# Another order for the seven quadrant products of a feed-forward layer on Trainium2

## The chip, the core and the metric

The kernel runs on one core of a Trainium2 chip. Five engines work side by side, each with its own stream of instructions: TensorE (PE in the profile; its weight loads are PEld), VectorE (DVE), ScalarE (ACT), GpSimd (POOL) and SyncE (SP), which here issues the transfers between HBM and the on-chip memory (SBUF). Matrix products land in PSUM, in banks of 128 x 512 floats. The metric is the device time of one execution in microseconds (us), and lower is better.

## The reference, cut to what matters

The program is one layer of an encoder over two independent sequences of 512 tokens with 1024 features: a state-space branch, a differential attention and a cross attention side by side, a gated sum of the three, and a gated feed-forward network. The change touches the last of these alone:

```python
x = x + merged @ p['w_out'][l]
xn2 = _rmsnorm(x, p['norm_ffn'][l])
gate, up = jnp.split(xn2 @ p['w_ffn_in'][l], 2, axis=-1)
return x + (jax.nn.silu(gate) * up) @ p['w_ffn_out'][l]
```

The hidden width is 2816, that is 22 tiles of 128. Everything is float32.

## The kernel before, in words

**Precision.** TensorE multiplies float32 values rounded to a shorter form. To keep float32 accuracy each operand is split into a high part (`split`, L128: a cast on ScalarE) and a low part (L129: the difference, on VectorE), and each product takes three matmuls: high x high, high x low, low x high. In the profile the moving halves are `th` and `tl`, the weight halves `wh` and `wl`.

**Quadrants.** The feed-forward products are computed two by two blocks at a time with seven block products instead of eight (Winograd's form of Strassen's method). For a hidden tile i the weights are A11 and A12 (two halves of the gate weights) and A21 and A22 (two halves of the up weights); the block sums are S1 = A21 + A22, S2 = S1 − A11, S3 = A11 − A21 and S4 = A12 − S2. The columns are the two sequences. The moving operands were split and summed earlier into seven slots, and `SEVEN` (L1006) pairs each weight block with its slot and sets the order of the products. One product of 128 x 512 is 4 k-steps x 3 = 12 matmuls.

**FF1** is the loop over the 22 hidden tiles. `weights4` (L939 to L970) loads the two weight tiles of i (buffers `wf`), splits A11 and A12 together and A22 alone, has POOL form the four sums (L959 to L962, S1 and S2 in one buffer `ws`, S3 and S4 in another, both of the four rotating `ld` buffers), and splits S12 and S34. S12 and S34 each have one pair of `wh`/`wl` buffers to themselves, so their split for tile i + 1 waits until the products of tile i that read them are over; A11/A12 and A22 share another two pairs in the same way. `products` (L1008) issues the matmuls: for i = 0 six products fill six banks together and the seventh follows; for i = 1 to 20 one product after another; for i = 21 the k loop is outermost, so that seven banks fill together, 21 matmuls per k-step. PSUM has six banks for products (`bkmm`) and two others (`bktr`), of which one takes the seventh product where seven fill together. A bank is free again when its last reader is done.

`quadrants` (L1041) combines the seven products p with sums on VectorE, all recorded at L1038: u2 = S2's product + p1 (p1 is ScalarE's copy of A11's product), c11 = A12's + p1, u3 = S3's + u2, u4 = S1's + u2, c22 = S1's + u3, c21 = A22's + u3, c12 = S4's + u4. c11 and c12 are the gate for the two sequences, c21 and c22 the up half. S1's bank is read twice. Then each sequence goes through the gate: VectorE multiplies by the norm factor (L1090), ScalarE takes tanh (L1091), POOL scales the up half (L1092), VectorE finishes (L1093, L1094), and the tile goes out to HBM (`aD`, L1095).

Beside this, from i = 1 to 18, the loop prepares pieces of the second layer's weights: raw weights are loaded, split, summed on POOL (L424 to L427) and split again, and written to HBM as `wD`.

**The turn to FF2.** At i = 21 the first two pairs of activation tiles are loaded again (`act_pair`, L1054: `fa` at L1057 and `fb` at L1058, in the same four `ld` buffers as the weight sums) and summed (`quad_sums`, L909, L911 and L912 on VectorE, L910 on POOL), then split.

**FF2** is 12 visits (`VISITS`), each to one row pair of outputs and a range of activation pairs, accumulating seven banks over the pairs; each pair is one pass of 21 matmuls with weights loaded from `wD` in two pieces (`prepared`, L1117, issued at L1126: A11, A12, A22 are 384 KB; S3, S2, S4, S1 are 512 KB). After a visit `quadrants` combines the banks and POOL adds the results to y (L1149); visits 0 to 3 also load x1 into y (L1139).

**Order.** TensorE keeps the program's order from i = 21 to the end of FF2. Elsewhere, and on all other engines, a scheduler that simulates the program chooses the order of the instructions on each engine, and of SP's transfers, so that a change of the program order also moves instructions that the edit doesn't name.

Of the kernel before, what the change touches and what calls it, by code (L numbers as in the profile page):

```python
# [14 lines left out]
ALU = mybir.AluOpType  # L15
# [5 lines left out]
L = 512  # L21
# [46 lines left out]
def encoder(ctx: ExitStack, tc: tile.TileContext, a, out):  # L68
    nc = tc.nc
    V, S, PO, PE = nc.vector, nc.scalar, nc.gpsimd, InOrder(tc, nc.tensor)  # L70
# [11 lines left out]
    def open_tags(es, side=None, **tags):  # L82

        for tag, n in tags.items():
            pools[tag] = es.enter_context(tc.tile_pool(name=tag, bufs=n, side=side, reuse_waits="tile"))
# [17 lines left out]
    def bank(tag="mm"):  # L103
        return pools[tag].tile([P, 512], F32, tag=tag, name="bk" + tag)

    def aux():
        return bank("tr")
# [29 lines left out]
    def weight(src, n=DM, tag=None):  # L137
        nonlocal last_w, last_s
        wf = wp.tile([P, DM], F32, tag="wf", name="wf")
        last_w = nc.sync.dma_start(wf[:, :n], src)  # L140
        wh, wl = (slot(tag, dt=F32R, name=n_) if tag else wp.tile([P, DM], F32R, tag=n_, name=n_) for n_ in ("wh", "wl"))
        last_s = split(wh[:, :n], wl[:, :n], wf[:, :n])
        return wh, wl
# [37 lines left out]
    def rstd(acc, n, nt=4):  # L181


        ss = aux()
        for t in range(nt):
            PE.matmul(ss[:, t : t + 1], acc[:, t * P : (t + 1) * P], onec[:, 0:1], start=(t == 0), stop=(t == nt - 1))
        return factor(ss, n, nt)
# [92 lines left out]
    @contextmanager  # L280
    def yielding(sp):

        with tc.issue_after(sp[0].ins), tc.issue_after(sp[1].ins):
            yield
# [145 lines left out]
    def half_piece(behind_=()):  # L430
        with ExitStack() as es_:
            for i_ in behind_:
                es_.enter_context(tc.issue_after(i_.ins))
            return next(prep, None)
# [189 lines left out]
    for i in range(-AHEAD, len(steps) + 1):  # L624
        if i + AHEAD < len(steps):
            h, s, lt = steps[i + AHEAD]
# [12 lines left out]
        if 0 <= i < len(steps):  # L639
            h, s, lt = steps[i]  # L640
# [8 lines left out]
        if i > 0 and steps[i - 1][2] == 3:  # L649
            h, s, _ = steps[i - 1]  # L650
# [318 lines left out]
    for i in range(3):  # L969
        for m in (i, i + 4):  # L970
            x1[m] = slot("x1", name=f"x1_{m}")
            w = weight(a["w_out"][m])
# [24 lines left out]
    def product(ps, w, o, ks=range(4)):  # L997
        wh, wl = w
        for k in ks:
            th, tl = ops[k]  # L1000
            ws_ = slice(k * P, (k + 1) * P)
            PE.matmul(ps, wh[:, ws_], th[:, o], start=(k == 0), stop=False)
            PE.matmul(ps, wh[:, ws_], tl[:, o], start=False, stop=False)
            PE.matmul(ps, wl[:, ws_], th[:, o], start=False, stop=(k == 3))

    SEVEN = (("A11", 0), ("S2", 4), ("A12", 1), ("S3", 5), ("S1", 3), ("A22", 6), ("S4", 2))  # L1006

    def products(i, w):  # L1008


        if i == 0:
            ps = [bank() for _ in range(6)]
            for j, k in ((0, 0), (0, 1), (1, 0), (1, 1), (0, 2), (1, 2), (0, 3), (1, 3)):
                for p_, (nm, o) in zip(ps, SEVEN):
                    if nm[0] == "AS"[j]:
                        product(p_, w[nm], o, (k,))
            yield from ps
            last = bank()
            product(last, w["S4"], 2)
            yield last  # L1020
        elif i == KFF - 1:
            ps = [bank() for _ in range(6)] + [aux()]
            for k in range(4):
                for p_, (nm, o) in zip(ps, SEVEN):
                    product(p_, w[nm], o, (k,))
            yield from ps
        else:
            for nm, o in SEVEN:
                p_ = bank()
                product(p_, w[nm], o)  # L1030
                yield p_
# [3 lines left out]
    def summed(tag, p_, other, bufs=1):  # L1035
        nonlocal last_sum
        t_ = (rp if tag == "nsq" else ap2).tile([P, L], F32, tag=tag, name=tag, bufs=bufs)
        last_sum = V.tensor_tensor(out=t_, in0=p_, in1=other, op=ALU.add)  # L1038
        return t_

    def quadrants(ps, p0, other=("up", "gf")):  # L1041

        p1 = ap2.tile([P, L], F32, tag="p1", name="p1")
        S.copy(p1, p0)
        u2 = summed("u2", next(ps), p1)
        c11 = summed("gf", next(ps), p1, 2)
        u3 = summed("u3", next(ps), u2)
        p5 = next(ps)
        u4 = summed("p1", p5, u2)
        c22 = summed("up", p5, u3, 2)  # L1050
        c21 = summed(other[0], next(ps), u3, 2)
        return c11, summed(other[1], next(ps), u4, 2), c21, c22

    def act_pair(p, tag="ts"):  # L1054

        xa_, xb_ = slot("ld", name="fa"), slot("ld", name="fb")
        nc.sync.dma_start(xa_, aD[2 * p])  # L1057
        nc.sync.dma_start(xb_, aD[2 * p + 1])  # L1058
        return xa_, xb_, quad_sums(xa_, xb_, tag)

    for i in range(KFF):
        w = res0
        if i > 0:
            wg = weights4(i)
            with yielding(last_q):
                w = next(wg)
            next(wg)
            next(wg)
        if i == 1:
            prep = prepare(pes, pieces[NPREP[1] :])  # L1070
            next(prep)
        elif i == KFF - 3:
            assert next(prep, None) is None
            pes.close()
            open_tags(fes, side="right", tsa=1, tsb=1)
        if i == KFF - 1:
            acts = [act_pair(0, "tsa"), act_pair(1, "tsb")]
            PE.on = True

        ps = products(i, w)  # L1080
        p0 = next(ps)
        if i == 0:
            for s in range(NS):
                _, bc = rstd(accs[s], DM)
                S.copy(accs[s], bc)
        gf0, gf1, up0, up1 = quadrants(ps, p0)
        ac = ap2.tile([P, NT], F32, tag="ac", name="ac")
        for s, gf, up in ((0, gf0, up0), (1, gf1, up1)):
            cs = slice(s * L, (s + 1) * L)
            V.tensor_tensor(out=gf, in0=gf, in1=accs[s], op=ALU.mult)  # L1090
            last_t = S.activation(out=ac[:, cs], in_=gf, func=AF.Tanh, scale=0.5)  # L1091
            PO.tensor_tensor(out=up, in0=up, in1=accs[s], op=ALU.mult)  # L1092
            V.scalar_tensor_tensor(out=ac[:, cs], in0=ac[:, cs], scalar=1.0, in1=gf, op0=ALU.add, op1=ALU.mult)  # L1093
            V.tensor_tensor(out=ac[:, cs], in0=ac[:, cs], in1=up, op=ALU.mult)  # L1094
        nc.sync.dma_start(aD[i], ac)  # L1095
        if 1 <= i < KFF - 3:
            half_piece((last_t, last_sum))
# [33 lines left out]
    for v, (m, lo_, hi_) in enumerate(VISITS):  # L1131
        ps = [bank() for _ in range(6)] + [aux()]
        for p in range(lo_, hi_):
            th, tl = pairs[p]
            w = prepared(m, p)
            if v < 4 and p == 1:
                with queued():
                    for t in (m, m + 4):
                        nc.sync.dma_start(y[t], x1D[t])  # L1139
            for p_, (nm, o) in zip(ps, SEVEN):  # L1140
                wh, wl = w[nm]
                PE.matmul(p_, wh, th[:, o], start=(p == lo_), stop=False)
                PE.matmul(p_, wh, tl[:, o], start=False, stop=False)
                PE.matmul(p_, wl, th[:, o], start=False, stop=(p == hi_ - 1))
        ps = iter(ps)
        c11, c12, c21, c22 = quadrants(ps, next(ps), ("nsq", "nsq"))
        for c_, t, s in ((c11, 0, 0), (c22, 4, 1), (c21, 4, 0), (c12, 0, 1)):
            yv = y[m + t][:, s * L : (s + 1) * L]
            PO.tensor_tensor(out=yv, in0=yv, in1=c_, op=ALU.add)  # L1149
        if v == 0:  # L1150
            with tc.issue_after(last_sum.ins):
                pairs.append(quad_split(2, *nxt))
        elif v == 1:
            with tc.issue_after(last_sum.ins):
                pair_in()
        for _ in range({3: 2, 4: 1, 6: 1, 7: 1}.get(v, 0)):
            pair_in()
        if v == 8:

            r0, r1 = quad_room(NPAIR)  # L1160
            r2 = slot("ts", [P, 4, L], F32R, name="r2")
            room = [(r0[:, 2 * i : 2 * i + 2], r1[:, 2 * i : 2 * i + 2]) for i in range(3)] + [(r2[:, 0:2], r2[:, 2:4])]
            ah, al = [], []
            for i in range(2 * NPAIR, KFF):
                ac = slot("ld", name="fl")
                nc.sync.dma_start(ac, aD[i])
                th, tl = (r_.rearrange("p a n -> p (a n)") for r_ in room[i - 2 * NPAIR])
                split(th, tl, ac, scale=0.5)
                ah.append(th)
                al.append(tl)  # L1170
# [472 lines left out]
```

## Time and profile before

| what | value |
|---|---|
| median of 3 runs | 1638.84 us (1638.17 to 1641.62) |
| the profiled execution | 1642.78 us, span 1641.0 us |
| TensorE busy | 1594.0 us, 97% of the span, 7812 matmuls |
| VectorE busy | 1176.3 us, 72% |
| ScalarE busy | 635.9 us, 39% |
| POOL busy | 551.3 us, 34% |
| mean granted TensorE clock | 0.99 |
| DMA, mean over the span | 158 GB/s |

The span is the profiled execution's own length on the core, and the time of that execution stands above it by what lies around the program. A line of the timeline gives the start in us, the duration, the engine and line (L1038 is line 1038 of the kernel), the operation, and output <- inputs with buffer numbers left out; square brackets give the idle time before the instruction and what ended it. "x2" marks instructions drawn together. A line of the waits gives who waited for whom, then the total in us, the number of times, and the longest. The granted clock is the share of full speed that TensorE was allowed.

### The profile page before, as it was taken

Reading aid. Unit: us, or ns where it says so; the run is one execution under the profiler, and the core shown is the slowest. Engines: PE = TensorE matmul, PEld = TensorE weight load, DVE = VectorE, ACT = ScalarE, POOL = GpSimd, SP = SyncE. Lnnn points to the kernel's source line nnn. Section 1 sums busy time; section 2 is a strip of 40 time slices with the busy share of each in tenths; the row PEclk is TensorE's granted clock in tenths of the full one; section 3 lists DMA queues with packets and bytes.
Section 4 is the critical chain, followed back from the end, with each engine's and each line's share of the span. In section 5 each row is a group of like instructions: output and inputs, shape, how many; then the busy total and the mean of one; then the engine's idle time right before and its main releaser. Section 6 shows DMA issues by size and latency. Waiting matters only on the chain.

```text
span 1641.0 us, 21700 instructions
## 1 busy us (share of the span) xinstructions
PE 1594.0 (97%) x7812; PEld 1315.9 (80%) x7812; DVE 1176.3 (72%) x1860; ACT 635.9 (39%) x1132; POOL 551.3 (34%) x444
## 2 busy tenths in 40 slices
PE   7999999899999999999999999999999998999997
PEld 5788787788898778777767887888888887888887
DVE  7957898246764676767567659998988887986445
ACT  6534323245553355564232444332333332331122
POOL 0001100000232221200565245666676664444242
PEclk9999999999999999999999999999999999999999
DMA  9354532746764110144785442333333334897632
GB/s 361 129 164 147 154 133 94 234 156 216 245 234 141 52 59 21 50 150 163 247 299 180 154 141 70 114 114 120 119 107 118 106 113 136 299 315 244 209 118 103
DMA packets 109354, 259.60 MB, mean 158 GB/s; under 512 B 14016, under 2 KB 42432, under 8 KB 109248
## 3 DMA queue, kind: packets, MB, share of 16 engines
q1 hardware_dynamic: 109248, 258.23, 46.6%
q8 instruction: 61, 1.00, 0.3%
q14 instruction: 45, 0.37, 0.1%
HBM read 174.85 MB, written 83.33 MB: 157 GB/s over the span
## 4 chain that ended last, share of the span: by engine, by line
PE 85%; DVE 6%; issue 3%; POOL 2%; DMA 2%; ACT 1%; SPq 0%; DVEq 0%; POOLq 0%; ACTq 0%
PE bkmm L61 74%; PE bktr L61 3%; PE bksc L61 2%; PE bkoo L61 2%; PE bktr L64 2%; PE bktr L1480 1%; DVE wl L129 1%; POOL mg L726 1%; PE bktr L1451 1%; DVE xt L243 0%; POOL up L1092 0%; DMA yt<-bD 0%; PE bktr L1419 0%; DMA c_r<-cD 0%; DVE tl L129 0%
## 5 line engine op out<-in xcount | busy, mean ns | idle before, releaser
L61 PE MATMUL bkmm<-xh,wh 128*128 128x512 f32 x640 | 255.9, 400 | 1.2 <-ACT wh L128 1.2
L61 PE MATMUL bkmm<-xh,wl 128*128 128x512 f32 x640 | 251.3, 393 | 2.3 <-DVE wl L129 2.3
L61 PE MATMUL bkmm<-xl,wh 128*128 128x512 f32 x640 | 251.1, 392 | 0.0
L61 PE MATMUL bkmm<-th,wl 128*128 128x512 f32 (+1 forms) x621 | 241.8, 390 | 4.8 <-DVE wl L129 4.8
L61 PE MATMUL bkmm<-th,wh 128*128 128x512 f32 (+1 forms) x621 | 241.6, 389 | 1.3 <-ACT th L128 1.3
L61 PE MATMUL bkmm<-tl,wh 128*128 128x512 f32 (+1 forms) x621 | 241.6, 389 | 0.2 <-DVE tl L129 0.2
L129 DVE TENSOR_TENSOR wl<-wf,wh 128x1024 fp32r<-128x1024 f32 (+1 forms) x133 | 148.1, 1113 | 86.9 <-ACT wh L128 77.7
L128 ACT CAST wh<-wf 128x1024 fp32r<-128x1024 f32 (+1 forms) x133 | 117.7, 885 | 205.7 <-PE bkmm L61 128.4
L424 POOL TENSOR_TENSOR raw<-raw 128x128 f32<-128x128 f32 x36 | 22.3, 620 | 391.9 <-DVE hl L132 388.4
L61 PEld LDWEIGHTS bkmm<-xh,wh 128*128 128x128 f32 x640 | 120.6, 188 | 32.0 <-issue 7.9
L61 PEld LDWEIGHTS bkmm<-xh,wl 128*128 128x128 f32 x640 | 120.3, 188 | 29.6 <-DVE wl L129 3.2
L61 PEld LDWEIGHTS bkmm<-th,wl 128*128 128x128 f32 x621 | 116.9, 188 | 29.3 <-DVE wl L129 5.5
L61 PE MATMUL bkmm<-th,w 128*128 128x512 f32 x432 | 139.8, 390 | 0.2 <-DVE up L1038 0.2
L61 PEld LDWEIGHTS bkmm<-xl,wh 128*128 128x128 f32 x640 | 120.7, 189 | 22.4 <-issue 0.4
L61 PEld LDWEIGHTS bkmm<-th,wh 128*128 128x128 f32 x621 | 116.9, 188 | 25.2 <-ACT th L128 1.4
L61 PEld LDWEIGHTS bkmm<-tl,wh 128*128 128x128 f32 x621 | 116.9, 188 | 24.8 <-DVE tl L129 0.6
L1092 POOL TENSOR_TENSOR up<-up,acc 128x512 f32<-128x512 f32 x44 | 84.1, 1930 | 90.5 <-DVE up L1038 90.5
L61 PEld LDWEIGHTS bkmm<-th,w 128*128 128x128 f32 x432 | 81.1, 188 | 18.8 <-DVE up L1038 1.5
L132 DVE SCALAR_TENSOR_TENSOR hl<-raw,hl 128x384 fp32r<-128x384 f32 (+1 forms) x72 | 73.8, 1029 | 24.6 <-ACT hl L131 24.5
L487 ACT ACTIVATE e<-bksc,nb 128x512 f32<-128x512 f32 (+1 forms) x96 | 58.8, 616 | 69.6 <-DVE nb L482 51.7
L61 PE MATMUL bkmm<-tl,w 128*128 128x512 f32 x216 | 84.1, 389 | 0.0
L61 PE MATMUL bkmm<-yh,wh 128*128 128x512 f32 x192 | 77.8, 406 | 3.9 <-DVE gl L722 3.9
(628 smaller groups left out, 3532.6 us busy)
## 6 DMA issues: line engine op xcount, KB each, us to landing
wf<-in_w_in SPq DMA_DIRECT2D x40, 512.0 KB, 4.1
wD<-hl SPq DMA_DIRECT2D x36, 512.0 KB, 2.9
w<-wD SPq DMA_DIRECT2D x36, 512.0 KB, 4.7
wD<-hl SPq DMA_DIRECT2D x36, 384.0 KB, 3.0
w<-wD SPq DMA_DIRECT2D x36, 384.0 KB, 3.8
gD<-gt SPq DMA_DIRECT2D x24, 512.0 KB, 2.9
gl<-gD SPq DMA_DIRECT2D x24, 512.0 KB, 4.0
wf<-in_w_fg SPq DMA_DIRECT2D x22, 512.0 KB, 3.6
```

The lines of the kernel that those rows point to most:

```text
L61: return self.put(self.eng.matmul(*args, **kw))
L64: return self.put(self.eng.transpose(*args, **kw))
L128: h = S.copy(hi, src)
L129: l_ = V.tensor_tensor(out=lo, in0=src, in1=hi.bitcast(F32), op=ALU.subtract)
L132: l_ = V.scalar_tensor_tensor(out=lo, in0=src, scalar=scale, in1=hi.bitcast(F32), op0=ALU.mult, op1=ALU.subtract)
L424: PO.tensor_tensor(out=a22, in0=a21, in1=a22, op=ALU.add)
L487: last_x = S.activation(out=e, in_=sc, func=AF.Exp, bias=nb, scale=scale, accum_out=sm)
L726: PO.tensor_tensor(out=mg[m], in0=mg[m], in1=gt, op=ALU.add)
L1092: PO.tensor_tensor(out=up, in0=up, in1=accs[s], op=ALU.mult)
L1451: PE.matmul(kp[64 * hf : 64 * hf + 48, g * 144 : (g + 1) * 144], l_[:, 2 * hf + g, :], o_[:, 4 * g4 + 2 * hf + g, :], start=(l_ is lr48), ...
L1480: PE.matmul(ps[:, g * P : (g + 1) * P], w_[:, gg * P : (gg + 1) * P], u_[:, 8 * o + gg, :], start=True, stop=True)
```

## The change

The seven products are issued in another order. Before it was A11, S2, A12, S3, S1, A22, S4; now it is A11, S2, A12, S1, S3, S4, A22. So S1 and S2, which share a buffer, are both read by the fourth product (before: the fifth), S3 and S4 by the sixth (before: the seventh), and A22 is read last (before: sixth). For i = 0 the product that follows the six is A22 instead of S4. `quadrants` takes the sums in the order that follows: u4 before u3, and c12 (a gate) before c21 (an up half). The gate loop is parted in two: first both gates (L1090, L1091, L1093), then the up halves, sequence 1 first. In FF2 the y sums take c12 before c21. No instruction is added or removed.

```diff
-    SEVEN = (("A11", 0), ("S2", 4), ("A12", 1), ("S3", 5), ("S1", 3), ("A22", 6), ("S4", 2))
+
+    SEVEN = (("A11", 0), ("S2", 4), ("A12", 1), ("S1", 3), ("S3", 5), ("S4", 2), ("A22", 6))
...
-            product(last, w["S4"], 2)
+            product(last, w["A22"], 6)
...
         c11 = summed("gf", next(ps), p1, 2)
-        u3 = summed("u3", next(ps), u2)
         p5 = next(ps)
         u4 = summed("p1", p5, u2)
+        u3 = summed("u3", next(ps), u2)
         c22 = summed("up", p5, u3, 2)
-        c21 = summed(other[0], next(ps), u3, 2)
-        return c11, summed(other[1], next(ps), u4, 2), c21, c22
+        c12 = summed(other[1], next(ps), u4, 2)
+        return c11, c12, summed(other[0], next(ps), u3, 2), c22
...
-        for s, gf, up in ((0, gf0, up0), (1, gf1, up1)):
+        for s, gf in ((0, gf0), (1, gf1)):
             cs = slice(s * L, (s + 1) * L)
             V.tensor_tensor(out=gf, in0=gf, in1=accs[s], op=ALU.mult)
             last_t = S.activation(out=ac[:, cs], in_=gf, func=AF.Tanh, scale=0.5)
+            V.scalar_tensor_tensor(out=ac[:, cs], in0=ac[:, cs], scalar=1.0, in1=gf, op0=ALU.add, op1=ALU.mult)
+        for s, up in ((1, up1), (0, up0)):
+            cs = slice(s * L, (s + 1) * L)
             PO.tensor_tensor(out=up, in0=up, in1=accs[s], op=ALU.mult)
-            V.scalar_tensor_tensor(out=ac[:, cs], in0=ac[:, cs], scalar=1.0, in1=gf, op0=ALU.add, op1=ALU.mult)
             V.tensor_tensor(out=ac[:, cs], in0=ac[:, cs], in1=up, op=ALU.mult)
...
-        for c_, t, s in ((c11, 0, 0), (c22, 4, 1), (c21, 4, 0), (c12, 0, 1)):
+        for c_, t, s in ((c11, 0, 0), (c22, 4, 1), (c12, 0, 1), (c21, 4, 0)):
```

## The prediction

> **What bounds the kernel now.** I read the page's shares first (TensorE is busy 97% of the span), then a table of windows over the FFN, then TensorE's waits from 874 us on, then the timeline where those waits lie. The columns of the windows are the stretch, its length, busy time of PE, PEld, DVE, ACT and POOL, granted clock, DMA share and GB/s.
>
> ```profile
> 960.00:1010.00 50.00, 48.49 (x226) 40.02 (x225) 39.88 (x41) 24.64 (x31) 27.84 (x18) 1.00 0.32 97
> 1010.00:1360.00 350.00, 350.00 (x1546) 289.82 (x1545) 309.68 (x335) 110.20 (x148) 227.94 (x148) 1.00 0.33 114
> 1384.00:1400.00 16.00, 11.17 (x41) 8.67 (x40) 9.53 (x13) 4.44 (x7) 4.62 (x3) 0.79 0.41 132
> 1400.00:1500.00 100.00, 99.77 (x438) 81.55 (x438) 84.16 (x101) 26.13 (x33) 46.33 (x32) 1.00 0.87 305
> 1500.00:1582.00 82.00, 82.00 (x362) 67.65 (x361) 42.10 (x56) 17.00 (x22) 27.51 (x22) 1.00 0.61 207
> ```
>
> ```profile
> PE bkmm L61 <- DVE wl L129: 7.1, 2, 4.8
> PE bkmm L61 <- ACT th L128: 1.3, 1, 1.3
> ```
>
> The reader is to see that the steady FF1 loop (1010 to 1360) has no idle TensorE time at all: reordering work there can gain nothing. The one large hole that the change can touch is in 1384 to 1400: 16 − 11.17 = 4.83 us, at a clock of 0.79. It belongs to the last tile, i = 21, whose k loop is outermost, so that all seven weight quadrants are wanted within its first 21 matmuls. Its timeline:
>
> ```profile
> 1375.80 0.69 DVE L909 TENSOR_TENSOR ts<-fa 128x512 f32<-128x512 f32 x1 [2.75 <-DMA fa<-aD]
> 1377.66 1.04 ACT L128 CAST wh<-ws 128x1024 fp32r<-128x1024 f32 x1
> 1380.34 0.62 ACT L128 CAST wh<-wf 128x512 fp32r<-128x512 f32 x1 [1.63 <-PE bkmm L61]
> 1382.85 1.21 DVE L129 TENSOR_TENSOR wl<-ws,wh 128x1024 fp32r<-128x1024 f32 x1
> 1383.09 1.05 ACT L128 CAST wh<-ws 128x1024 fp32r<-128x1024 f32 x1 [2.13 <-PE bkmm L61]
> 1384.09 0.32 SPq L1057 DMA_DIRECT2D fa<-aD  x1
> 1384.59 1.18 DVE L129 TENSOR_TENSOR wl<-wf,wh 128x512 fp32r<-128x512 f32 x1
> 1385.15 0.39 PE L61 MATMUL bkmm<-th,wh 128*128 128x512 f32 x1
> 1385.38 0.40 PE L61 MATMUL bkmm<-tl,wh 128*128 128x512 f32 x1
> 1386.92 0.69 DVE L1094 TENSOR_TENSOR ac<-ac,up 128x512 f32<-128x512 f32 x1 [1.15 <-POOL up L1092]
> 1388.13 0.68 DVE L909 TENSOR_TENSOR ts<-fa 128x512 f32<-128x512 f32 x1
> 1389.33 1.22 DVE L129 TENSOR_TENSOR wl<-ws,wh 128x1024 fp32r<-128x1024 f32 x1
> 1390.58 0.32 SPq L1058 DMA_DIRECT2D fb<-aD  x1
> 1390.60 0.79 PE L61 MATMUL bkmm<-th,wl 128*128 128x512 f32 x1 [4.83 <-DVE wl L129]
> ...
> 1394.59 0.40 PE L61 MATMUL bktr<-th,wl 128*128 128x512 f32 x1
> ```
>
> S3's low half (the `wl` at 1389.33) ends the hole. Its high half could be cast only at 1383.09, when S4, the seventh product of i = 20, had let the S34 buffer go; A22's cast at 1380.34 follows the sixth. On VectorE the low half then stands behind `ac*up` (which waits for POOL), a sum, L909 and a gate.
>
> **The hole at i = 21 goes.** What it costs: matmuls normally start 0.23 us apart (1385.15, 1385.38); the next started at 1390.60, so 4.99 us were lost. The nine steps from 1390.60 to 1394.59 took 3.99 us (0.44 each) where nine of 0.227 take 2.04, so 1.95 us more went. (0.227 us is the loop's 350.00 us over its 1546 matmuls.) Together **6.94 us**. [...]
>
> With the change S34 is let go by the sixth product, 12 matmuls x 0.227 = 2.72 us sooner. S12 (cast at 1377.66) is let go by the fourth instead of the fifth, also 2.72 sooner, at 1374.94; in the new order its low half follows L909 on fa0 (1375.80) and ends, with a sum between, at about 1378.05. Then SP issues the load of fa1 (before, it followed that low half at 1384.06 by 0.03 us), which lands 4.0 to 5.6 us later by this group of issues:
>
> ```profile
> fa<-aD SPq DMA_DIRECT2D x7, 512.0 KB, 4.3
> fb<-aD SPq DMA_DIRECT2D x7, 512.0 KB, 5.6
> ```
>
> L909 on fa1, one gate multiply and S34's low half follow (0.6 + 0.6 + 1.2 = 2.4 us). With 4.3 it is done at 1384.8; TensorE wanted it at 1385.61 before, with the fourth product; S3 is now the fifth, three matmuls later: 1386.29. A22, now last, is cast after the seventh product and is ready at 1387.2 to 1387.8, against a want, two products on, of 1386.29 + 1.36 = 1387.65. So 0 to 1 us is left: I take 0.2. The cover is fa1's landing: if it takes over 1386.29 − 2.4 − 1378.05 = 5.8 us, the hole comes back one for one. **−6.94 + 0.2 = −6.74.**
>
> **The loop, i = 1 to 20: nothing.** Every instruction is there as often as before, in another order; the row 1010:1360 shows VectorE busy 309.68 of 350 and POOL 227.94, so both keep some slack. S34 comes free earlier; A22, S34's former place, has 2.72 us more wait for its buffer, but its split is two half-size instructions (0.62 and 1.18 us, above) and is used only 16 us later. S1's bank, now fourth, is read by two sums (u4, c22), but comes round again after six products. If this cover failed, each 0.1 us per tile would cost 20 x 0.1 = 2 us. POOL's two multiplies now stand behind the next tile's four sums, with one tile (19.03 us) of room. SP's store of the gated tile goes after the wD store and a second load; its reader is far away. Three loads of activation tables at i = 0 become one, off TensorE's path: 0.
>
> **The start, i = 0 and 1: +0.65.** Six banks are full together at i = 0, and i = 1's third product takes the bank that held i = 0's fourth. That was S3 (one reader, u3, third sum); now S1, whose last reader c22 is the fifth. Two sums later at 0.6 us each is 1.2; before, TensorE lost 50 − 48.49 = 1.51 us in that window but none here, so some slack hides part of it. Ends 0 and 1.3; I take the middle, 0.65.
>
> **The turn to FF2 (start of visit 0): +1.6.** Each visit refills seven banks in product order, three matmuls (0.68 us) each. If a visit's first matmul starts at S, the bank that held S1 is wanted at S + 2.72 before (fifth), at S + 2.04 after (fourth). Its last reader is c22 of the stage before.
>
> ```profile
> 1397.16 0.69 DVE L911 TENSOR_TENSOR ts<-fb,ts 128x512 f32<-128x512 f32 x1 [5.29 <-DMA fb<-aD]
> 1407.50 0.68 DVE L1038 TENSOR_TENSOR u<-bkmm,p 128x512 f32<-128x512 f32 x1
> 1409.12 0.39 PE L61 MATMUL bkmm<-th,w 128*128 128x512 f32 x1
> 1411.13 1.28 DVE L1038 TENSOR_TENSOR up<-bkmm,u 128x512 f32<-128x512 f32 x2
> 1411.62 0.75 PE L61 MATMUL bkmm<-th,w 128*128 128x512 f32 x2
> ```
>
> Before, VectorE runs without a gap from fb1's landing (1397.16) to u2 (1407.50), 10.34 us; c22, the first of the pair at 1411.13, ends at 1411.81 = S + 2.69, and two matmuls at 1411.62 took 0.75 instead of 0.62: 0.13 lost. After, S is 1409.12 − 6.94 = 1402.18. fb1 is issued when S34's low half ends (1384.8 to 1385.3), lands 5.6 to 6.6 later (6.58 before, 1390.58 to 1397.16), and 10.34 later u2 starts: 1400.7 to 1402.2. Six instructions (u2, c11, u3, u4, a gate, L909) at 0.6 and c22's 0.68 follow: c22 ends between S + 2.8 and S + 4.3, against a want of S + 2.04. Stall 0.8 to 2.4, and a little more for the handing over; I take 1.7, less the 0.13: **+1.57**.
>
> **Later visits: +1.8.** The first two rows are the sums of visit 0, then come those of visits 2, 3, 4 and 7, each behind S of the visit that follows:
>
> ```profile
> 1421.43 0.68 DVE L1038 TENSOR_TENSOR up<-bkmm,u 128x512 f32<-128x512 f32 x1
> 1422.16 0.50 PE L61 MATMUL bkmm<-th,w 128*128 128x512 f32 x1 [0.23 <-DVE up L1038]
> 1448.14 0.39 PE L61 MATMUL bkmm<-th,w 128*128 128x512 f32 x1
> 1449.37 0.68 DVE L1038 TENSOR_TENSOR up<-bkmm,u 128x512 f32<-128x512 f32 x1
> 1467.18 0.39 PE L61 MATMUL bkmm<-th,w 128*128 128x512 f32 x1
> 1469.01 0.68 DVE L1038 TENSOR_TENSOR up<-bkmm,u 128x512 f32<-128x512 f32 x1
> 1481.49 0.39 PE L61 MATMUL bkmm<-th,w 128*128 128x512 f32 x1
> 1483.46 0.68 DVE L1038 TENSOR_TENSOR up<-bkmm,u 128x512 f32<-128x512 f32 x1
> 1524.45 0.39 PE L61 MATMUL bkmm<-th,w 128*128 128x512 f32 x1
> 1526.49 0.68 DVE L1038 TENSOR_TENSOR up<-bkmm,u 128x512 f32<-128x512 f32 x1
> 1526.94 0.79 PE L61 MATMUL bkmm<-th,w 128*128 128x512 f32 x2
> ```
>
> The wait at 1422.16, with uneven steps beside it, cost 0.71 us in all; the new stall at visit 0 gives VectorE more time than that, so it goes: −0.71. The other four c22 end at S + 1.91, 2.51, 2.65 and 2.72; the last cost 0.17 (0.79 instead of 0.62), so the bank is in truth wanted some 0.17 ahead of the matmul: at S + 2.55 before, S + 1.87 after. In the new order c12 goes ahead of c22 at visits 2 and 7 (+0.6), at 3 and 4 c22 keeps its place: they end at S + 2.51, 2.51, 2.65 and 3.32, 0.64, 0.64, 0.78 and 1.45 late. A stall at one visit gives VectorE, busy 84.16 of 100 here, time before the next, so for 3 and 4 I take half: 0.64 + 0.32 + 0.39 + 1.45 − 0.10 and 0.17 that visits 4 and 7 lost before = +2.5; ends 0 (VectorE reaches its sums early) and 3.5 (the full sum, less those two, with nothing halved is 3.24). With −0.71: **+1.82**. POOL's y sums keep their number and have room (46.33 of 100). The larger weight piece is often issued ahead of the smaller, as A22 is read last; the pieces are three passes of 21 x 0.227 = 4.76 us deep: 0.
>
> **Sum.** −6.74 + 0 + 0.65 + 1.57 + 1.82 = **−2.7 us**. The profiled execution is 1642.78 (span 1641.0 and 1.78 around it), 3.94 above the median of 1638.84; I carry the difference over: 1638.84 − 2.7 = **1636.1**.
>
> **Rivals.** *Nothing comes back*: hole gone, no new wait: −6.74 − 0.13 − 0.71 − 0.27 = −7.85, **1631.0**. For it: VectorE idles 16 us per 100 in the visits. Against: by the rows above c22 ends beyond its new due time at four visits.
>
> *The hole moves to visit 0*: L909 waits for fa1 ahead of S34's low half, so fb1, issued after it, is late twice over. If fa1 takes the 5.6 of fb, S34 ends 1.3 later, fb1 lands 1.3 later and the stall at visit 0 is 1.7 + 1.3 = 3.0, sum −1.4; with fb1 at its longest too, 4.0: sum −0.4, **1638.4**. A stall of this size might bring the slow clock, at 1.94 more (**1640.3**); 1.30 us waited for `th` in 960:1010 left it at 1.00. [...]
>
> *Slower: weights late in the saturated stretch.* SP now issues visit 0's two y loads ahead of two weight pieces, and 1400:1500 has DMA at 0.87 and 305 GB/s. 1 MB of y at 305 GB/s is 3.4 us; w pieces land in under 7.3 here and are asked for up to three passes ahead. If TensorE waits for w at each of the four visits that load y, it decides from 1.6 us each (6.4 in all; −2.7 + 6.4 = +3.7): **1642.5**. Against: no wait for w in 1400 to 1500 before.
>
> *Nothing happens*: the loop is bound by TensorE's 350.00 of 350 and the matmuls are unchanged; true but for the hole.
>
> **How the numbers follow.** Forecast 0.42 (own range 1633.5 to 1638.5, from its terms' ends), nothing comes back 0.20, hole moves 0.18, weights late 0.20. About 0.2% (3.28 us, so 1635.56 and 1642.12) is what a measurement of this kernel tells from no change. Faster: 0.20 + 0.20 of the forecast = 0.40. Same: 0.22 of the forecast, 0.12 of the moved hole = 0.34. Slower: 0.06 of the moved hole, if it brings the slow clock and the visits at their upper end, and 0.20 = 0.26. Range 1631.0 to 1643.0: the clean gain to the late weights.
>
> **What would show it.** Right: no wait for `wl` near 1385; 1384:1400 all busy, clock 1.00; new waits of TensorE for `up` L1038 at four or five visit starts, some 1 to 2 us at visit 0. Wrong: a wait for `wl` at i = 21 behind L909 and `fa`; waits for `w<-wD`; holes in 1010:1360.

## The result, and the profile after

The changed kernel takes 1647.14 us (median of 10 runs). The kernel before, measured beside it in 10 runs, takes 1641.8 us. The ratio is **1.0029, 95% interval 1.0017 to 1.0041: slower by 0.29%, some 4.8 us**. One of the ten runs of the changed kernel took 3569.44 us and is left out of the ratio. The prediction said 1636.1 and a gain of 2.7. Of the 11.0 us between 1636.1 and 1647.14, 3.0 are the starting time (1638.84 from three runs, 1641.8 from ten); the rest is the change.

The profiled execution after took 1648.34 us with a span of 1645.7, against 1642.78 and 1641.0 before. Windows of the kernel after, in the columns that the prediction explains. (Line numbers move: L1038 of the kernel before is L1039 in the kernel after, the gate's lines are L1091 to L1093, L1096 and L1097, the store of the gated tile is L1098, and the edits of the experiments move them further.)

```profile
1010.00:1360.00 350.00, 348.41 (x1534) 286.45 (x1533) 281.02 (x327) 107.24 (x147) 186.53 (x145) 1.00 0.32 108
1384.00:1400.00 16.00, 11.99 (x39) 7.83 (x38) 15.37 (x17) 3.24 (x4) 9.28 (x7) 0.79 0.34 112
1400.00:1500.00 100.00, 99.77 (x440) 82.07 (x439) 85.24 (x101) 29.66 (x37) 44.39 (x30) 1.00 0.87 306
1500.00:1582.00 82.00, 82.00 (x363) 67.92 (x362) 40.88 (x55) 14.73 (x19) 31.56 (x25) 1.00 0.63 212
```

TensorE is no longer busy for all of the steady loop, the hole at 1384 to 1400 is still there with its clock of 0.79, and FF2 has no new holes. What TensorE waited for in the kernel after (us in total, times, longest), first from 1010 to 1370, then from 1370 to 1410:

```profile
PE bkmm L61 <- DVE wl L129: 1.6, 3, 0.6
```

```profile
PE bkmm L61 <- DVE wl L129: 2.0, 2, 1.5
PE bkmm L61 <- DVE u L1039: 1.8, 1, 1.8
PE bkmm L61 <- DVE up L1039: 0.2, 1, 0.2
```

The starts of the matmuls tell more than the waits, because after a wait the next starts are uneven (in the kernel after, 0.34 and then 0.24 us apart behind the wait that ended at 1391.61, against 0.227 in the loop) and after some the clock is low (0.79 in 1384:1400). From the first matmul of i = 2 to the first of i = 21 the kernel before took 361.76 us (1021.28 to 1383.04), the kernel after 364.99 (1022.58 to 1387.57): the loop lost 3.2 us, nearly all of it at waits for weights near 1178, 1216, 1255 and 1295 us (before: none). By the steps over 0.227 us per matmul, the hole at i = 21 cost 7.6 us (before: 6.9). I split the profiled executions at the first matmul of FF1, the first of FF2 and the last of FF2. FF1 took 430.66 us before (978.46 to 1409.12) and 434.85 after (979.49 to 1414.35); FF2 took 172.43 and 171.79; the rest behind it 59.45 and 59.53. So **the whole loss of the change is in FF1, +4.2 us**: 3.2 in the loop, 0.7 at the hole, 0.3 at i = 0 and 1. FF2 took 0.65 less, which is within what it differs by where its order is as before (171.47 and 172.79 in experiments 6 and 7). What lies ahead of FF1 isn't touched, and differs by up to 5 us from one profiled execution to the next (FF1 began at 974.2 to 979.5 in all that follow), which is why the FF1 time is given beside the medians below.

**The loop after.** One turn of it, from one load of w_fu to the next, in the order of time (timelines of SP, POOL, ScalarE and VectorE):

```profile
1205.19 0.47 SPq L945 DMA_DIRECT2D wf<-in_w_fu  x1
1210.44 1.29 POOL L959 TENSOR_TENSOR ws<-wf 128x512 f32<-128x512 f32 x1 [5.83 <-DMA wf<-in_w_fu]
1212.94 1.74 POOL L960 TENSOR_TENSOR ws<-ws,wf 128x512 f32<-128x512 f32 x1
1214.72 1.05 ACT L128 CAST wh<-ws 128x1024 fp32r<-128x1024 f32 x1 [2.39 <-POOL ws L960]
1215.81 1.34 DVE L129 TENSOR_TENSOR wl<-ws,wh 128x1024 fp32r<-128x1024 f32 x1 [1.67 <-ACT wh L128]
1217.07 0.68 DVE L1039 TENSOR_TENSOR u<-bkmm,u 128x512 f32<-128x512 f32 x1
1218.39 0.68 DVE L1039 TENSOR_TENSOR gf<-bkmm,p 128x512 f32<-128x512 f32 x1
1219.11 1.28 DVE L1091 TENSOR_TENSOR gf<-gf,acc 128x512 f32<-128x512 f32 x1
1220.42 0.63 ACT L1092 ACTIVATE ac<-gf 128x512 f32<-128x512 f32 x1 [3.28 <-DVE gf L1091]
1221.38 0.60 ACT L128 CAST wh<-wf 128x512 fp32r<-128x512 f32 x1
1223.12 1.78 DVE L129 TENSOR_TENSOR wl<-wf,wh 128x512 fp32r<-128x512 f32 x1
1224.93 0.33 SPq L945 DMA_DIRECT2D wf<-in_w_fu  x1
```

Each row waits for the one above it, on another engine or in its own engine's order, with a few other instructions of the same engine between: the load lands, POOL forms S1 and S2, S12 is split, the sums that VectorE takes behind that split follow, then the second gate and its tanh, and only then, behind the tanh on ScalarE, A22 is cast and its low half computed. That low half is the last reader of the w_fu buffer, so the next load starts 0.03 us after it. This turn took 19.74 us; ten turns from 1049.55 to 1244.15 took 19.46 each, and the first six of them, up to 1166.35, took 19.47 each, though TensorE had not waited yet. TensorE needs 19.04 per tile (its tiles start that far apart before). **The tile has become a closed chain that is longer than its matmuls**, TensorE's lead melts by 0.4 us per tile, and when it is gone the waits begin (the one of this turn, up to 1217.20, is for S12's low half, the row at 1215.81).

Before, the same load was never on such a chain. In the timelines of the kernel before:

```profile
1189.94 0.62 ACT L128 CAST wh<-wf 128x512 fp32r<-128x512 f32 x1 [1.35 <-PE bkmm L61]
1192.60 0.33 SPq L945 DMA_DIRECT2D wf<-in_w_fu  x1
1206.29 1.05 ACT L128 CAST wh<-ws 128x1024 fp32r<-128x1024 f32 x1 [0.34 <-PE bkmm L61]
```

A22's cast was released by TensorE, with the sixth product, for the next tile; and S12's cast came 13.7 us after the load and waited for TensorE as well, not for the load. With A22 last, its buffers come free only when the tile is over, so A22 is split a whole tile later, in the tile that uses it, and the raw weights hold their buffer until then.

**The hole after.** At the turn to FF2 the load of w_fu for i = 21 was issued 10.4 us ahead of that tile's first matmul (1377.20 and 1387.57); before, 20.1 us ahead (1362.91 and 1383.04). That load and what hung on it:

```profile
1377.20 0.33 SPq L945 DMA_DIRECT2D wf<-in_w_fu  x1
...
1384.75 1.74 POOL L960 TENSOR_TENSOR ws<-ws,wf 128x512 f32<-128x512 f32 x1
1386.53 1.05 ACT L128 CAST wh<-ws 128x1024 fp32r<-128x1024 f32 x1 [2.71 <-POOL ws L960]
1388.23 1.05 ACT L128 CAST wh<-ws 128x1024 fp32r<-128x1024 f32 x1 [0.65 <-POOL ws L961]
1389.33 0.50 PE L61 MATMUL bkmm<-th,wl 128*128 128x512 f32 x1 [0.47 <-DVE wl L129]
1391.61 0.50 PE L61 MATMUL bkmm<-th,wh 128*128 128x512 f32 x1 [1.78 <-DVE u L1039]
1395.19 1.21 DVE L129 TENSOR_TENSOR wl<-ws,wh 128x1024 fp32r<-128x1024 f32 x1
1396.46 0.80 PE L61 MATMUL bkmm<-th,wl 128*128 128x512 f32 x1 [1.54 <-DVE wl L129]
1398.51 0.63 PE L61 MATMUL bktr<-th,wh 128*128 128x512 f32 x1
```

S34's cast at 1388.23 now waits for POOL's sum, not for a product; letting its buffer go 2.72 us sooner could not help, since nothing was there to be split. From S12's low half (it starts at 1387.61) to S34's at 1395.19 VectorE has no gap over 0.1 us, so S34's low half also stands in VectorE's queue, and TensorE's wait of 1.78 us is for a bank that a late sum (u3) still read.

### The profile page after: what moved, and what is told of

The parts are those of the page before. It is cut to its first block, busy times and chain, and to the rows that moved or that the text cites. A ratio compares the mean times of both kernels' runs of the same rounds, so it can differ in the third digit from the quotient of the medians.

```text
span 1645.7 us, 21661 instructions
## 1 busy us (share of the span) xinstructions
PE 1596.5 (97%) x7812; PEld 1315.3 (80%) x7812; DVE 1156.5 (70%) x1860; ACT 631.4 (38%) x1130; POOL 512.2 (31%) x444
## 4 chain that ended last, share of the span: by engine, by line
PE 66%; DVE 15%; POOL 6%; DMA 6%; issue 4%; ACT 2%; SPq 0%; DVEq 0%; POOLq 0%; ACTq 0%
PE bkmm L61 54%; DVE wl L129 4%; DMA wf<-in_w_fu 3%; PE bktr L61 3%; PE bksc L61 2%; PE bkoo L61 2%; PE bktr L64 2%; POOL mg L726 2%; DVE st L1501 1%; POOL ws L960 1%; POOL ws L959 1%; ACT wh L128 1%; POOL ws L962 1%; DMA raw<-in_w_fo 1%; DVE gf L1091 1%
## 5 line engine op out<-in xcount | busy, mean ns | idle before, releaser
L129 DVE TENSOR_TENSOR wl<-wf,wh 128x1024 fp32r<-128x1024 f32 (+1 forms) x133 | 161.9, 1217 | 85.7 <-ACT wh L128 77.0
L1096 POOL TENSOR_TENSOR up<-up,acc 128x512 f32<-128x512 f32 x44 | 65.1, 1481 | 125.3 <-DVE up L1039 113.2
L1092 ACT ACTIVATE ac<-gf 128x512 f32<-128x512 f32 x44 | 27.7, 632 | 197.9 <-DMA aD<-ac 128.3
L129 DVE TENSOR_TENSOR wl<-ws,wh 128x1024 fp32r<-128x1024 f32 x44 | 56.1, 1275 | 41.9 <-ACT wh L128 41.9
```

What stands on the lines that cost most here:

```text
L129: l_ = V.tensor_tensor(out=lo, in0=src, in1=hi.bitcast(F32), op=ALU.subtract)
```

## The experiments

**1. A22 back to sixth.** Is it A22's place, or S1's?

```diff
-    SEVEN = (... ("S1", 3), ("S3", 5), ("S4", 2), ("A22", 6))
+    SEVEN = (... ("S1", 3), ("S3", 5), ("A22", 6), ("S4", 2))
```

with the last product of i = 0 and the last two sums put back accordingly; the parted gate loop and the new y sums stay.

> The changed kernel with A22 sixth and S4 last again (S1 stays fourth, S3 fifth). Theory, A22 last closes a loop: in the changed kernel A22 of tile i is split only while tile i runs, so the w_fu buffer is let go a tile later, and the chain w_fu load, POOL's sums, S12's split, the sums on VectorE, the second tanh, A22's split, next w_fu load takes 19.3 to 19.7 us per tile against 19.03 of matmuls. Here A22 is split a tile ahead again: w_fu loads 18.7 to 19.0 us apart, no wait for wl between 1170 and 1300 us (2.8 us in the changed kernel), the hole at i = 21 about 7 us as before, in all 0 to +1 us on the kernel before. Rival, S1 as fourth product (its bank read twice, the sums in the other order) costs the time: it stays 4 to 5 us slower than before.

Measured: 1644.2 us, ratio to before 1.0019 (1.0009 to 1.0028). The loop behaves as the theory says: no wait at all from 1010 to 1370, w_fu loads 19.04 us apart (1076.34 to 1266.71, ten turns). The total does not: FF1 took 432.53, 1.9 us more than before. It is at the turn, where the hole grew from 6.9 to 8.7 us:

```profile
PE bkmm L61 <- DVE wl L129: 5.8, 2, 5.1
PE bkmm L61 <- DVE u L1039: 0.7, 1, 0.7
```

So A22's place closes the loop, and with S4 as the seventh product the hole stays. It even grew, because VectorE takes the sums and splits there in another order: S34's low half came 9.12 us after its cast began (1378.84 to 1387.96), against 6.24 before (1383.09 to 1389.33). Whether S1 ahead of S3 or the parted gate loop brought that order is not shown. The median is 3.2 us above before, 1.3 more than FF1 accounts for; whether that is more than the spread of what lies ahead of FF1 isn't settled.

**2. The new order only where the hole is**, for i = 20, 21 and in FF2; gates as before.

```diff
+    NEW_AT = (KFF - 2, KFF - 1)
+    def seven(i):
+        return SEVEN_B if i in NEW_AT else SEVEN_A
...
-            for nm, o in SEVEN:
+            for nm, o in seven(i):
...
+    gf0, gf1, up0, up1 = quadrants(ps, p0, new=i in NEW_AT)
```

(`SEVEN_A` is the old order, `SEVEN_B` the new one, and `quadrants` takes the sums to match.)

> Old product order and sums for i = 0 to 19, the new ones for i = 20, 21 and in FF2; the gate loop as before. Theory of the loop: tiles up to 19 run as before (no waits), w_fu of i = 21 is loaded early, S34 is let go by the sixth product of i = 20, so the hole at i = 21 falls from 6.9 to 0 to 3 us, and the kernel is 4 to 7 us faster than before. Rival, the new order itself makes the hole (VectorE's order at the turn): hole 6 to 8 us, time within 2 us of before or slower.

Measured: 1638.53 us, 0.9983 (0.9975 to 0.9992), 2.8 us faster; FF1 428.16. The loop is as before. The hole fell from 6.9 to 4.5 us, less than expected: two short waits (1.1 for `wl`, 1.3 for a bank that a late sum still read) and the slow clock that followed (0.70 from 1385 to 1390). S34 is cast sooner, as predicted, but its low half comes 5.81 us after the cast began, because five other instructions of VectorE (L912, three sums and a gate's multiply) stand between S12's low half and it:

```profile
1377.83 1.05 ACT L128 CAST wh<-ws 128x1024 fp32r<-128x1024 f32 x1 [1.51 <-PE bkmm L61]
1383.64 1.21 DVE L129 TENSOR_TENSOR wl<-ws,wh 128x1024 fp32r<-128x1024 f32 x1
```

The new order does what the prediction said at the place it said, in part: 2.4 us of the 6.7.

**3. A22 split without waiting.** A22 fills only half of its buffers, so two tiles' A22 fit in one pair; A11 and A12 keep the other.

```diff
+        if i == 0:
+            own["A11"] = [wp.tile([P, DM], F32R, tag=t_, name=t_) for t_ in ("wh", "wl")]
+            own["A22"] = [wp.tile([P, DM], F32R, tag=t_, name=t_) for t_ in ("wh", "wl")]
...
+            else:
+                c0 = i % 2 * H if names[0] == "A22" else 0
+                wh, wl = (t_[:, c0 : c0 + n] for t_ in own[names[0]])
```

(The other branch of the `else`, for S12 and S34, is the line as it was.)

> The changed kernel with the splits of A22 in alternate halves of one pair of buffers that is held for the whole loop (A11 and A12 in the other pair), so that A22 of tile i + 1 need not wait for the product of tile i. Nothing else is edited. Theory of the loop: A22 is split a tile ahead, w_fu loads come at least 8 us earlier against the matmuls, no waits in the loop, the hole shorter by 3 us or more: 3 to 8 us faster than the changed kernel. Rival, another link (VectorE's order, S1's bank): as the changed kernel, within 1.5 us.

Measured: 1647.11 us, 1.0037 (1.0023 to 1.0051); FF1 438.82. A miss: as slow as the changed kernel, with more waits in the loop (3.9 us; the profiled execution, 1650.92, is the slowest of the six runs). Its timelines show another closed chain:

```profile
1248.33 0.33 SPq L1108 DMA_DIRECT2D aD<-ac  x1
```

```profile
1254.31 0.63 ACT L1102 ACTIVATE ac<-gf 128x512 f32<-128x512 f32 x1 [10.49 <-DMA aD<-ac]
1254.85 1.99 ACT L128 CAST wh<-ws 128x1024 fp32r<-128x1024 f32 x2
```

The gated tile `ac` has one buffer. The first tanh of a tile waits until the store of the tile before has landed, and the casts of S12 and S34 stand behind that tanh on ScalarE. In the new order the two up halves are finished last, so the store goes out late: a second loop through the same sums, 19.79 us per turn here (w_fu loads at 1074.88 and ten turns on at 1272.74). Why that is more than the 19.46 of the changed kernel, in which this wait for the store stands as well (`aD<-ac`, 108.2 us of ScalarE's idle time from 1050 to 1360), is not shown; the edit also moves other instructions. Experiments 4 and 5 test the two loops.

**4. Two buffers for `ac`, alone.**

```diff
+    open_tags(fes, side="right", acb=1)
...
-        ac = ap2.tile([P, NT], F32, tag="ac", name="ac")
+        ac = slot("acb", name="ac") if i % 2 == 0 else ap2.tile([P, NT], F32, tag="ac", name="ac")
```

> The changed kernel with two buffers for the gated tile ac (even and odd tiles), so that the first tanh of a tile need not wait for the store of the tile before. Nothing else. Theory: two loops run through the tile in the changed kernel, one through the w_fu buffer (A22's split lets it go), one through ac (store, first tanh, S12's split behind it on ScalarE, the sums, the second tanh, the up halves, the store). Cutting the second alone leaves the first: w_fu loads still 19.3 to 19.6 us apart between 1040 and 1300 us, loop waits 1 to 3 us, time within 2 us of the changed kernel. If ac alone is the loop: w_fu loads 19.03 apart, no waits, 3 to 5 us faster than the changed kernel.

Measured: 1643.07 us, 1.0011 (1.0002 to 1.0021), 4 us below the changed kernel; FF1 432.42. The w_fu loads are 19.24 us apart (1064.61 to 1257.03): the first loop is still the longer one, if only by 0.2 us per turn, and i = 2 to 20 lost 0.6 us in all. The hole stayed, at 7.8 us. The time moved more than expected, the spacing less.

**5. Both cuts**, with the order of the changed kernel: the two edits of experiments 3 and 4 together, on the changed kernel.

```diff
+                wh, wl = (t_[:, c0 : c0 + n] for t_ in own[names[0]])
...
+        ac = slot("acb", name="ac") if i % 2 == 0 else ap2.tile([P, NT], F32, tag="ac", name="ac")
```

> Both cuts: A22's splits in alternate halves and two buffers for ac; products, sums and gates as in the changed kernel. Theory of the two loops: no wait for wl between 1020 and 1370 us (2.8 us in the changed kernel, 5.1 with the halves alone), w_fu loads 19.03 us apart, and the hole at i = 21 shorter by 2 us or more than the 7.6 of the changed kernel: as fast as the kernel before or up to 6 us faster. Rival, it is not the buffers but the engines' order (VectorE and ScalarE work in an order that ties S12's split to the sums): waits stay over 2 us and the time stays 4 us or more above before.

Measured: **1635.06 us, 0.9966 (0.9952 to 0.9979): by that ratio 5.6 us faster than before**, 12 us faster than the changed kernel, and the fastest of all. Windows of this kernel:

```profile
1010.00:1360.00 350.00, 350.00 (x1546) 289.83 (x1545) 325.01 (x337) 110.08 (x149) 206.29 (x148) 1.00 0.34 115
1370.00:1400.00 30.00, 30.00 (x134) 24.79 (x133) 27.69 (x34) 13.32 (x16) 4.39 (x3) 1.00 0.48 162
```

Both loops are cut, the w_fu loads follow at 18.87 us (1071.07 to 1259.79), TensorE has no hole in the loop, and **the hole at i = 21 is gone with its slow clock**: from 1010 to 1582 us the only wait is 0.2 us. FF1 took 423.87, 6.79 less than before.

**6. One link of the chain made longer**: the second gate's tanh issued twice, in the changed kernel and, as a control, in the one before.

```diff
+            if s == 1:
+                last_t = S.activation(out=ac[:, cs], in_=gf, func=AF.Tanh, scale=0.5)
```

> The changed kernel with the second gate's tanh issued twice (same result, 0.55 to 0.63 us more on ScalarE per tile, on the chain named above). Theory of the loop: the chain is the loop's limit, so the tile takes 0.5 to 0.6 us longer: w_fu loads 19.9 to 20.2 us apart, 6 to 11 us slower than the changed kernel. Rival, the loop is bound by TensorE and the waits come from elsewhere: ScalarE is busy 107 of 350 us, so 0.6 us more cost nothing, within 1.5 us of the changed kernel.

> The kernel before with the second gate's tanh issued twice, as a control: there no chain through a tile is as long as its matmuls (w_fu loads follow TensorE at 19.03 us with slack), so both theories expect no change in the loop: 0 to +1 us on the kernel before (up to 0.6 at the turn to FF2).

Measured: 1657.99 us in the changed kernel, 1.0102 on before (1.0084 to 1.0119), 10.9 us above the changed kernel; 1639.67 in the kernel before, 0.9985 (0.9973 to 0.9997). The window of the loop in the first:

```profile
1010.00:1360.00 350.00, 342.13 (x1488) 278.57 (x1487) 271.66 (x316) 112.89 (x159) 181.78 (x142) 1.00 0.32 106
```

ScalarE works 113 of 350 us there, yet 0.6 us more on it cost 0.75 us per tile (w_fu loads 20.21 apart, 1069.35 to 1271.43, against 19.46). An engine with two thirds of its time free sets the pace, because it stands on the chain. In the kernel before the same instruction cost nothing in the loop; the hole came out 1.4 us shorter, which I had not expected. The rows of that control show where from:

```profile
1381.00 1.05 ACT L128 CAST wh<-ws 128x1024 fp32r<-128x1024 f32 x1 [2.15 <-PE bkmm L61]
1386.10 1.22 DVE L129 TENSOR_TENSOR wl<-ws,wh 128x1024 fp32r<-128x1024 f32 x1
1387.23 0.68 DVE L1090 TENSOR_TENSOR gf<-gf,acc 128x512 f32<-128x512 f32 x1
```

The second gate's multiply, which stood ahead of S34's low half before (1388.73, then 1389.33), now stands behind it, and the low half comes 5.10 us after its cast began instead of 6.24.

**7. The old order with both cuts.** Is the order needed for the gain? The same two edits, on the kernel before:

```diff
     SEVEN = (("A11", 0), ("S2", 4), ("A12", 1), ("S3", 5), ("S1", 3), ("A22", 6), ("S4", 2))
+                wh, wl = (t_[:, c0 : c0 + n] for t_ in own[names[0]])
...
+        ac = slot("acb", name="ac") if i % 2 == 0 else ap2.tile([P, NT], F32, tag="ac", name="ac")
```

> The kernel before (old order of products and sums) with the same two cuts as the fast version: A22's splits in alternate halves, two buffers for ac. Theory: with the old order S34's split for i = 21 still waits for the seventh product of i = 20, so the hole at i = 21 stays at 4.5 us or more plus the slow clock, no loop waits as before, and the time is within 2 us of the kernel before; then the gain needs the new order and the cuts together. Rival, the cuts alone take the hole away: 4 us or more faster than before.

Measured: 1637.35 us, 0.9973 (0.9961 to 0.9985); FF1 425.94. The expectation failed: the cuts alone take most of the hole. One wait is left, and the clock did not fall behind it (the matmuls from 1387.02 on started 0.23 us apart):

```profile
1386.68 0.50 PE L61 MATMUL bkmm<-th,wl 128*128 128x512 f32 x1 [2.01 <-DVE wl L129]
1387.02 0.39 PE L61 MATMUL bkmm<-th,wh 128*128 128x512 f32 x1
```

S34 still waits for the seventh product there, but on VectorE its low half comes at 1385.41, 3.35 us after its cast began; before it came 6.24 us after (1383.09 to 1389.33), behind more work: A22's low half, which stood between them (1384.59), now comes a tile earlier (1361.06). So the hole of the kernel before was partly the buffer that the change lets go sooner, and for the larger part VectorE's queue at that place; which of the two cuts shortens the queue is not tested. On top of the cuts the new order takes away the last wait, 2.1 us of FF1 in these two profiled executions (425.94 to 423.87). The ratios, 0.9973 and 0.9966, do not tell the two kernels apart, since their intervals overlap.

**8. FF2 alone** in the new order, FF1 as before:

```diff
-            for p_, (nm, o) in zip(ps, SEVEN):
+            for p_, (nm, o) in zip(ps, SEVEN_B):
                 wh, wl = w[nm]
...
-        for c_, t, s in ((c11, 0, 0), (c22, 4, 1), (c21, 4, 0), (c12, 0, 1)):
+        for c_, t, s in ((c11, 0, 0), (c22, 4, 1), (c12, 0, 1), (c21, 4, 0)):
```

> FF1 as before, the new order of products, sums and y sums in FF2 alone. The prediction's bank step (S1's bank wanted by the fourth product of the next visit) expects new waits for up at the starts of visits 3, 4, 5 and 8, 2 to 3.5 us in all. Rival, banks go to the next visit in the order in which they come free, so S1's bank goes to the fifth or sixth product: no new wait over 0.5 us, time within 1 us of before.

Measured: 1640.55 us, 0.9995 (0.9985 to 1.0004). Behind the hole at i = 21 there is no wait of TensorE in FF2 at all. The new order costs nothing there. FF1, whose order this edit leaves alone, took 431.39 here against 430.66 before, so FF1 times that differ by less than some 0.7 us are not told apart.

## Why the prediction was wrong, step by step

**The loop, "i = 1 to 20: nothing": wrong, and the main cause of the slowdown.** It makes 3.2 of FF1's 4.2 us, and the late loads at the turn follow from it. The step weighed whether A22's split would be *ready in time for its product* ("used only 16 us later"), which it always was. It did not ask what the split lets go: the buffer of w_fu, whose next load starts the next tile's sums. It also passed over the store of the gated tile ("its reader is far away"), whose landing frees `ac` for the next tanh. Both waits close a chain from tile to tile. "VectorE busy 309.68 of 350" was no proof of slack, as the doubled tanh shows: a chain that passes through three engines and a transfer can be longer than the tile while each of them has time free (VectorE 281.02 of 350 in the kernel after, POOL 186.53, ScalarE 107.24). Measured: 19.46 us per turn instead of 19.04, 3.2 us lost in the loop, and a used-up lead at the turn. The sign that the prediction gave for this, "holes in 1010:1360", came.

**The hole, −6.74: wrong, right only in that S34's buffer is let go sooner.** In the changed kernel the hole came out 0.7 us longer (7.6 against 6.9). The step computed from the time at which S12's buffer is let go (1374.94) and took for granted that the sums to be split were there. They were not: POOL's S12 sum ended at 1386.49. Where the sums are there, the order takes 2.4 us of the hole (experiment 2), since VectorE has more ahead of S34's low half than the sum, L909 and one gate multiply that the step counted; behind the cuts it takes 2.1 (experiment 7). That FF1 falls by 6.79 us with both cuts, the size predicted, is luck: 4.7 of it come from the cuts in the old order (430.66 to 425.94). The cover that the step named (fa1's landing) was not what failed: the load was issued at 1389.31, and L909 read it at 1393.42, within the 5.8 us allowed.

**The start, +0.65: 0.3 came, not for the reason given.** From the first matmul of i = 0 to the first of i = 2 it took 42.83 us before and 43.09 after, which lies within the ends of the step and within what two executions differ by. From 960 to 1020 us TensorE waited for `tl` (1.9 us in two waits; before, 1.3 for `th` and 0.2 for `tl`) and never for a bank that a sum still read.

**The turn to FF2 and the visits, +1.57 and +1.82: wrong, both from one step**, "the bank that held S1 is wanted by the fourth product". Measured: 0.6 us at visit 0 and none after it, where the kernel before had lost 1.1 in all. The rows of the kernel after around visit 3 show why:

```profile
1453.01 0.39 PE L61 MATMUL bkmm<-th,w 128*128 128x512 f32 x1
1454.83 0.62 PE L61 MATMUL bkmm<-th,w 128*128 128x512 f32 x2
```

```profile
1455.18 0.68 DVE L1039 TENSOR_TENSOR up<-bkmm,u 128x512 f32<-128x512 f32 x1
```

The fourth product began nine matmuls after 1453.01, at 1455.05 (the second of the pair at 1454.83), and did not wait, though c22 read S1's bank until 1455.86. So it was not in that bank. The reading that fits all visits, though the rows do not name the banks: a bank goes to the next visit in the order in which it comes free, and c22's goes to the fifth or sixth product. What visit 0 waited for (1418.20, behind c12's `gf`) was the sixth product's bank.

**Rivals.** The one that ended slower (weights late in the saturated stretch) did not happen: there is no wait for `w` behind 1400 us. The true mechanism was none of them: it lay in the loop that the prediction had closed with "can gain nothing", which is right, and from which it concluded that nothing could be lost there either.

## What to carry to other kernels

When an operand moves to the end of a tile, ask not only when it is needed but what its preparation lets go; a split that frees a load's buffer is part of the next tile's chain. Follow each single buffer once round the loop (load, use, store, next load) and add the durations: where the sum comes near the bound engine's time per tile, a reordering that costs no work can still cost time, whatever the busy shares say (in the kernel after 19.46 us per turn against 19.04, with VectorE, the busiest engine beside TensorE, at 281.02 of 350 us). And a gain that is missing may be waiting behind such a loop: with two buffers freed, the same order was 5.6 us faster than before, though 4.4 of these came with the buffers alone, in the old order.

## What the runs showed of the hardware

**The clock fell without one long idle stretch, and not always after the same one.** At the hole after, no single wait is over 1.78 us, yet from 1393.44 the matmuls started 0.43 us apart and the clock of 1384:1400 is 0.79. One wait of 2.01 us (experiment 7) did not bring it. And one and the same wait of 2.3 us, ahead of FF1, is followed by slow matmuls in some executions and not in others. Before, then after:

```profile
874.00:960.00 86.00, 85.79 (x371) 70.82 (x372) 51.38 (x56) 32.68 (x39) 32.79 (x20) 0.98 0.48 154
```

```profile
874.00:960.00 86.00, 83.41 (x366) 68.74 (x367) 53.09 (x55) 33.07 (x39) 33.40 (x21) 1.00 0.50 159
```

The wait was 2.31 us long in the one (up to 874.21) and 2.30 in the other (up to 876.22). In nine of the eleven profiled executions (one of each kernel; those of experiments 1 and 8 are not counted) it was 2.29 to 2.32 us. Six of the nine show the slow matmuls behind it (0.43 us apart, some 1.5 us lost in all: before, experiments 3 to 5 and both of 6), and three do not (after, experiments 2 and 7), which would make part of the spread between runs. So a single wait of 2.3 us was enough in six executions and not in three; what decides it is not shown. The prediction said of a stall of 3.0 to 4.0 us that it might bring the slow clock; no execution had such a stall at visit 0, so the runs do not test that.

**Some instructions of VectorE and POOL took longer where they overlapped.** In the turn shown above POOL's sum takes 1.29 us while VectorE idles (1210.44), and a sum of the same size 1.74 when it overlaps VectorE's work (1212.94). Shortly before the turn to FF2 VectorE took 1.78 us for the first of the two products that finish a tile, beside a POOL multiply of 1.67 (1376.65 to 1378.32), and 0.67 for the second (in the kernel after):

```profile
1377.09 2.38 DVE L1097 TENSOR_TENSOR ac<-ac,up 128x512 f32<-128x512 f32 x2
```

The first of the two ended at 1378.88, 0.55 us behind POOL's multiply. VectorE's sums that read a bank did not slow down: the 59 of L1039 that overlap POOL by over 0.3 us between 1010 and 1400 us took 0.68 on average and 0.69 at most. Such stretches lie on the chain too.
